# The place of the blocks' triangular inversion in the mixers' step order of a hybrid decoder layer

## The chip, the cores and the metric

The program runs on one core of one Trainium2 chip. The metric is the device time of one execution in microseconds (us); the time of the kernel before is the median of three runs. The profile is one further execution, with its own time. The engines are named as in the profile: PE multiplies matrices, PEld is PE's loading of the stationary operand, DVE and ACT do elementwise work, POOL is a slower elementwise engine, SP issues the DMAs.

## The reference

One layer of a decoder works on 1040 tokens (16 learned meta tokens and 1024 others) of width 1024, in float32:

```
h = h + 0.5 * swiglu(rmsnorm(h))                     # feed-forward 1
u = rmsnorm(h);  p = u @ w_in                        # one combined projection
o_a = gated DeltaNet(p), 8 heads of 128 x 128, chunks of tokens
o_b = RWKV-7 time mixing(p), 16 heads of 64 x 64
h = h + (sigmoid(ga) * o_a + sigmoid(gb) * o_b) @ w_out
h = h + 0.5 * swiglu(rmsnorm(h))                     # feed-forward 2
out = rmsnorm(h), without the meta tokens
```

Inside a chunk of the DeltaNet, the delta rule asks for the inverse of a unit lower triangular matrix:

```
m = where(strict, (k*beta) @ k.T * decay, 0)
tinv = inverse(m + eye)                              # triangular solve
u = tinv @ (v*beta);  wk = tinv @ (k*beta*exp(g))
step: v_new = u - wk @ S;  o = (q*exp(g)) @ S + attn @ v_new;  S = S*exp(g_last) + k_tail.T @ v_new
```

The kernel brings the RWKV branch, in the reference a scan over the tokens, into the same chunked form, so it too needs such inverses. Everything else of the mixers (projections, convolution, gates, norms) feeds these two recurrences or closes them.

## The kernel before, in words

Feed-forward 1 comes first, then the part that this case is about (function `middle`), then feed-forward 2. The middle works on two halves of the sequence: the first half has 528 columns (the 16 meta tokens and 512 others), the second 512. Each half is worked in eight steps, one for each slice of 128 channels (one DeltaNet head and two RWKV heads), so there are sixteen steps, `it` = 0 to 15. A float32 weight tile is split into a high and a low part, and each projection is three products per slice of the contraction: 24 matmuls of 512 columns, or 24 of 272 and 24 of 256 for the 528 columns of the first half (`proj`, line 307, tile `pp`).

What a step does is a list of actions in a string (lines 187 to 192): one plus sign behind a name means the action works for the step after this one, two for the step after that. For a step `it` the actions are:

- `merge_blocks`: makes 64- and 128-wide inverses from the 32-wide ones by small products on PE (lines 1619, 1627, 1638, 1643, PSUM tiles `iv`).
- `transitions`: the RWKV chunk matrices (tiles `xp`, `mp`, `np`).
- `operands+`: the next step's products of keys and queries (`grb` and `gra` on PE; `LT` and `UA` on DVE); its helper `inverse_inputs` sends the 32-wide diagonal blocks to DRAM and brings them back into `Ub`, a block to a partition.
- `inverses+`: inverts the blocks of the next step. It is 31 pairs of DVE instructions (lines 1584 and 1586, tiles `tb` and `Xb`), each of which needs the one before, and a copy `Yt` (line 1587). Then SP writes `Xb` and `Yt` to DRAM (`scX`, line 1589; `scY`, line 1591) and reads them back in another layout: `Xc` (line 1594) and `Y` (line 1598). `Xc` is what the first product of `merge_blocks` reads, `Y` what its second reads. POOL copies a part of `Xc` into `XA` as it lands (line 1600).
- `chains`: the recurrences, four chunks of 128 and eight of 64, with short hops from PE to DVE or ACT and back (lines 1742 to 1768).
- `gates`: three projections and a small product; `finish`: norms and the closing of the step, its result to DRAM (line 1828).
- `decay++`, `new_b++`, `new_a++`: the projections and first operands for the step after the next. `new_b` has three projections, and at its end the product `bon` (two matmuls of 512 columns), which DVE turns into `bv` (line 1370). `new_a` has three projections, each followed by a short convolution on DVE (line 1393, tile `acc`), by sigmoids on ACT and by norms (products `cs` with `onesr`).

The order of the instructions on each engine is fixed when the program is built: a scheduler takes the traced instructions, lets what was traced earlier go ahead where both are ready by its own estimate of durations, and writes one queue for each engine. On the chip each engine then works through its queue in this order, so PE waits where the next matmul's operand is not there, even if a later one could go. `chains`, `finish` and `inverses` use DVE together. The weight tiles (`wraw`, 512 KB each, line 260) are loaded by the same SP queue that carries the inversion's transfers; there are two raw buffers and two split ones.

Step 0's inverses are made ahead of the loop (string `FIRST`), those of step 15 in step 14 (`LAST_BUT_ONE`). The strings `REGULAR` (steps 0 to 5 and 8 to 13), `BEFORE_SWITCH` (step 6, which also begins the second half) and `SWITCH` (step 7) order the rest.

Of the kernel before, what the change touches and what calls it, by code (L numbers as in the profile page):

```python
# [170 lines left out]
def schedule():  # L171
# [5 lines left out]
    for it in range(last + 1):  # L177
        order = {NJ - 2: BEFORE_SWITCH, NJ - 1: SWITCH, last - 1: LAST_BUT_ONE, last: FINAL}.get(it, REGULAR)
        for act in order.split():
# [5 lines left out]


FIRST = "decay new_b tokens new_a decay+ operands inverses new_b+ new_a+"
REGULAR = "merge_blocks transitions operands+ inverses+ chains gates finish decay++ new_b++ new_a++"
BEFORE_SWITCH = "merge_blocks transitions operands+ inverses+ chains gates finish banks gates+ segment decay++ new_b++ tokens++ new_a++"
SWITCH = "merge_blocks transitions operands+ inverses+ chains finish decay++ new_b++ new_a++"  # L190
LAST_BUT_ONE = "merge_blocks transitions operands+ inverses+ chains gates finish"
FINAL = "gates merge_blocks transitions chains fill finish"

# [1728 lines left out]
```

## Time and profile before

| | |
|---|---|
| median of 3 runs | 3003.53 us (2999.59 to 3004.59) |
| profiled execution | 3001.24 us, span 2999.5 us, mean granted clock 0.992 |
| PE busy | 2886.0 us, 96% of the span |
| DVE busy | 2189.7 us, 73% |
| ACT busy | 1445.4 us, 48% |
| POOL busy | 491.9 us, 16% |
| the sixteen merges | first product at 865.8 us of the span, last at 2236.8 us |

How to read it: shares of busy time are means over stages. The time of an engine in one step is read from the view by windows, the start of a group and what ended the idle time before it from the timeline, and the sums of waits from the view of waits. In a timeline a row is: start, us from its first start to its last end, engine, line, operation, tiles (out<-in), shapes, count, and in brackets the engine's idle time before it with what ended it. A matmul's own duration is its time through the array; what a row of n matmuls costs PE is read from the start of the next row. A float32 matmul (`iv`, `vap`, the chains) is run as two. SPq is SP's queue: there the length of a row is how long the issuing took, not the transfer.

### The profile page before, as it was taken

How to read it: one execution, taken by the hardware profiler on the slowest of the kernel's cores; microseconds unless marked ns; L12 is line 12 of the kernel's file. 1: busy time of each engine (PE TensorE's matmuls, PEld its weight loads, DVE VectorE, ACT ScalarE, POOL GpSimd, SP SyncE). 2: the span in 40 equal slices, each digit the busy share in tenths (PEclk: the TensorE clock that was granted, in tenths of full speed). 3: DMA queues.
4: the chain of work that ended last, by engine and by line, in shares of the span. 5: the costliest groups of instructions: out<-in, count | busy, mean ns of one | idle time of the engine just before them, and what ended most of it. 6: DMA issues, size and time to landing. Idle time of an engine off the chain costs nothing. (4 is left out here: it accounts for less than half of the span.)

```text
span 2999.5 us, 62835 instructions
## 1 busy us (share of the span) xinstructions
PE 2886.0 (96%) x25630; PEld 2497.4 (83%) x25630; DVE 2189.7 (73%) x4080; ACT 1445.4 (48%) x2546; POOL 491.9 (16%) x553
## 2 busy tenths in 40 slices
PE   8999999998989999999998999999999999999998
PEld 8999999998877888888776777777787888888886
DVE  7566668876668877788867887778866666667886
ACT  5322224436555656566566556656644432223444
POOL 0332332323000000000000100000100033332431
PEclk9999999999999999999999999999999999999999
DMA  3433236553232322333332332233354332323763
GB/s 124 135 107 103 96 116 212 190 184 109 72 74 67 80 71 67 82 81 86 93 91 72 81 82 71 75 87 86 106 139 169 113 106 102 103 102 132 249 221 106
DMA packets 286849, 333.14 MB, mean 111 GB/s; under 512 B 172432, under 2 KB 178576, under 8 KB 286560
## 3 DMA queue, kind: packets, MB, share of 16 engines
q1 hardware_dynamic: 284752, 325.77, 35.6%
q8 instruction: 201, 3.29, 0.5%
q10 hardware_dynamic: 1728, 3.16, 0.3%
q14 instruction: 88, 0.72, 0.1%
q0 software_dynamic: 80, 0.19, 0.0%
HBM read 261.67 MB, written 67.38 MB: 110 GB/s over the span
## 5 line engine op out<-in xcount | busy, mean ns | idle before, releaser
L307 PE MATMUL pp<-uk,w 128*128 128x512 f32 (+2 forms) x4824 | 968.7, 346 | 9.3 <-DVE w L164 5.7
L307 PEld LDWEIGHTS pp<-uk,w 128*128 128x128 f32 x4824 | 742.8, 190 | 106.0 <-DVE w L164 13.1
L707 PE MATMUL pd<-form,w 128*128 128x256 f32 (+2 forms) x2772 | 435.0, 318 | 5.2 <-DVE w L164 4.6
L707 PEld LDWEIGHTS pd<-form,w 128*128 128x128 f32 x2772 | 395.3, 188 | 44.4 <-DVE w L164 6.7
L494 PE MATMUL pg<-bt,w 128*128 128x256 f32 (+2 forms) x2520 | 401.6, 317 | 3.0 <-DVE w L164 2.0
L164 DVE TENSOR_TENSOR w<-wraw,w 128x1024 fp32r<-128x1024 f32 (+2 forms) x266 | 346.6, 1303 | 71.7 <-ACT w L163 68.3
L494 PEld LDWEIGHTS pg<-bt,w 128*128 128x128 f32 x2520 | 360.1, 188 | 37.1 <-DVE w L164 3.1
L163 ACT ACTIVATE w<-wraw 128x1024 fp32r<-128x1024 f32 (+2 forms) x266 | 276.3, 1040 | 188.1 <-PE pg L494 116.2
L500 DVE TENSOR_TENSOR c<-c,pg 128x520 f32<-128x520 f32 (+1 forms) x280 | 189.5, 688 | 238.7 <-PE pg L494 214.7
L494 PE MATMUL pg<-b,w 128*128 128x256 f32 (+2 forms) x2160 | 347.8, 317 | 0.0
L494 PEld LDWEIGHTS pg<-b,w 128*128 128x128 f32 x2160 | 309.7, 188 | 28.1
L163 ACT ACTIVATE w<-wrx 128x1024 fp32r<-128x1024 f32 (+1 forms) x64 | 58.4, 912 | 279.8 <-PE pg L494 237.3
L464 POOL TENSOR_TENSOR wrx<-wrx 128x512 f32<-128x512 f32 x38 | 52.5, 1382 | 722.9 <-DVE w22b L164 544.9
L163 ACT ACTIVATE w<-wsum 128x768 fp32r<-128x768 f32 x96 | 75.7, 789 | 154.9 <-PE pd L707 128.8
L164 DVE TENSOR_TENSOR form<-form 128x520 fp32r<-128x520 f32 (+1 forms) x152 | 141.2, 964 | 11.0 <-ACT form L163 10.6
L164 DVE TENSOR_TENSOR w<-wsum,w 128x768 fp32r<-128x768 f32 x96 | 117.9, 1232 | 36.7 <-ACT w L163 36.7
L163 ACT ACTIVATE form<-form 128x520 fp32r<-128x520 f32 (+1 forms) x152 | 94.6, 633 | 77.6 <-DMA form<-frm 64.6
L1586 DVE TENSOR_TENSOR Xb<-Xb,tb 115x126 f32<-115x126 f32 (+22 forms) x496 | 125.4, 253 | 9.0 <-DVE rhA L1744 0.2
L242 POOL TENSOR_TENSOR wsum<-wsum,wraw 128x768 f32<-128x768 f32 (+1 forms) x48 | 98.7, 2071 | 202.7 <-DMA wraw<-in_wdn 142.0
L1584 DVE TENSOR_TENSOR tb<-Ub,Xb 115x126 f32<-115x126 f32 (+22 forms) x496 | 124.1, 250 | 8.8 <-DMA Ub<-scr 1.6
L1393 DVE SCALAR_TENSOR_TENSOR acc<-xr,pk,acc 128x528 f32<-128x528 f32 (+1 forms) x144 | 108.9, 757 | 29.2 <-ACT acc L1389 28.6
L307 PE MATMUL pwo<-uk,w 128*128 128x512 f32 x384 | 98.7, 407 | 4.1 <-ACT w L163 3.3
(424 smaller groups left out, 4381.8 us busy)
## 6 DMA issues: line engine op xcount, KB each, us to landing
wraw<-in_win SPq DMA_DIRECT2D x150, 512.0 KB
wraw<-in_wgu SPq DMA_DIRECT2D x44, 512.0 KB
wrx<-in_wgu SPq DMA_DIRECT2D x44, 512.0 KB
frm<-c SPq DMA_DIRECT2D x76, 260.0 KB
form<-frm SPq DMA_DIRECT2D x76, 260.0 KB
frm<-c SPq DMA_DIRECT2D x76, 256.0 KB
form<-frm SPq DMA_DIRECT2D x76, 256.0 KB
wraw<-in_wdn SPq DMA_DIRECT2D x40, 384.0 KB
```

Of the source, the lines that this page charges most:

```text
L163: g.nc.scalar.activation(hi, src, AF.Copy)
L164: (eng or g.nc.vector).tensor_tensor(lo, src, hi.bitcast(F32), op=ALU.subtract)
L242: g.nc.gpsimd.tensor_tensor(s, x, y, op=ALU.add if r == 1 else ALU.subtract)
L307: g.nc.tensor.matmul(ps, lhsT=l, rhs=r, start=i == 0, stop=i == n - 1)
L464: sums.tensor_tensor(a22, a21, a22, op=ALU.add)
L494: nc.tensor.matmul(ps[:, c0 : c0 + cn], lhsT=l[:, x, k, :], rhs=r[:, k, y, c0 : c0 + cn], start=i == 0, stop=i == 3 * HK - 1)
L500: nc.vector.tensor_tensor(o, x, y, op=ALU.add)
L707: nc.tensor.matmul(pd[:, c0 : c0 + cn], lhsT=wd[:, u, k - k0, :], rhs=x[:, v, c0 : c0 + cn], start=k + i == 0, stop=k == HF - 1 and i == 2)
L1393: nc.vector.scalar_tensor_tensor(acc[:, :n], xr[:, tap : tap + n], V("convw", ct * 4 + tap), acc[:, :n], op0=ALU.mult, op1=ALU.add)
L1584: nc.vector.tensor_tensor(tv, U[:, i, i + 1 :].unsqueeze(2).to_broadcast([npt, nt, ncc]), X[:, i, 0:ncc].unsqueeze(1).to_broadcast([npt, n ...
L1586: nc.vector.tensor_tensor(X[:, i + 1 :, 0:ncc], X[:, i + 1 :, 0:ncc], tv, op=ALU.add)
```

## The change

In three of the strings the word `inverses+` stands at another place. In `REGULAR` and `SWITCH` it moves from behind `operands+` to between `new_b++` and `new_a++`; in `BEFORE_SWITCH` from behind `operands+` to behind `finish`. No instruction is added or removed; the priorities by which the scheduler orders the queues change.

```
-REGULAR = "merge_blocks transitions operands+ inverses+ chains gates finish decay++ new_b++ new_a++"
-BEFORE_SWITCH = "merge_blocks transitions operands+ inverses+ chains gates finish banks gates+ segment decay++ new_b++ tokens++ new_a++"
-SWITCH = "merge_blocks transitions operands+ inverses+ chains finish decay++ new_b++ new_a++"
+REGULAR = "merge_blocks transitions operands+ chains gates finish decay++ new_b++ inverses+ new_a++"
+BEFORE_SWITCH = "merge_blocks transitions operands+ chains gates finish inverses+ banks gates+ segment decay++ new_b++ tokens++ new_a++"
+SWITCH = "merge_blocks transitions operands+ chains finish decay++ new_b++ inverses+ new_a++"
```

Three places show what this does to the queues. The merge of step 4 stands for those of steps 3 to 6, whose rows are alike, and the merge of step 12 for those of steps 10, 12 and 14.

First place, DVE, the end of the inversion for step 4 (`tb`, `Xb`, `Yt`). Before, it ends ahead of the tail of `new_b` (from `rB` on), and the row of `bv` stands fifteen rows below the last one shown:

```order
L1584 TENSOR_TENSOR tb<-Ub,Xb 115x16
L1586 TENSOR_TENSOR Xb<-Xb,tb 115x16
L1587 COPY Yt<-Xb 115x512
L1130 SCALAR_TENSOR_TENSOR rB<-pp,pk,rB 128x528
L1363 TENSOR_TENSOR AR<-rB,ELx 128x8x64
L164 TENSOR_TENSOR w<-wraw,w 128x1024
```

Now the inversion runs on through `new_b` and into the first convolutions of `new_a`. These are the rows from `bv` on:

```order
L1370 TENSOR_TENSOR bv<-bon,vB 128x512
L1584 TENSOR_TENSOR tb<-Ub,Xb 115x70
L1393 SCALAR_TENSOR_TENSOR acc<-xr,pk,acc 128x528
L1586 TENSOR_TENSOR Xb<-Xb,tb 115x5x14
L164 TENSOR_TENSOR w<-wraw,w 128x1024
L1584 TENSOR_TENSOR tb<-Ub,Xb 115x56
L1437 COPY bkpm<-bkm 64x64
L1438 COPY bkpm<-bkm 64x64
L1586 TENSOR_TENSOR Xb<-Xb,tb 115x4x14
```

and these the ones that follow them, to the end of the inversion:

```order
L1584 TENSOR_TENSOR tb<-Ub,Xb 115x45
L1586 TENSOR_TENSOR Xb<-Xb,tb 115x3x15
L1584 TENSOR_TENSOR tb<-Ub,Xb 115x30
L1397 TENSOR_TENSOR acc<-acc,xr 128x528
L1586 TENSOR_TENSOR Xb<-Xb,tb 115x2x15
L1393 SCALAR_TENSOR_TENSOR acc<-xr,pk,acc 128x528
L1584 TENSOR_TENSOR tb<-Ub,Xb 115x16
L1393 SCALAR_TENSOR_TENSOR acc<-xr,pk,acc 128x528
L1586 TENSOR_TENSOR Xb<-Xb,tb 115x16
L164 TENSOR_TENSOR w<-wraw,w 128x1024
L1587 COPY Yt<-Xb 115x512
```

The last `Xb` has moved from 19 rows ahead of `bv` to 17 rows behind it.

Second place, PE, from the second `bon` to the first product of the merge of step 4 (`iv` from `Xc`). Before:

```order
L1216 MATMUL bon<-hl,bdr 128x512
L307 MATMUL pp<-uk,w 128x256 x14
L307 MATMUL pp<-uk,w 128x272 x24
L307 MATMUL pp<-uk,w 128x256 x16
L1216 MATMUL cs<-hl,onesr 128x256
L1216 MATMUL cs<-hl,onesr 128x272
L307 MATMUL pp<-uk,w 128x256 x8
L1619 MATMUL iv_14489<-Xc,LT 32x32
```

Now:

```order
L1216 MATMUL bon<-hl,bdr 128x512
L307 MATMUL pp<-uk,w 128x256 x21
L307 MATMUL pp<-uk,w 128x272 x24
L307 MATMUL pp<-uk,w 128x256 x8
L1216 MATMUL cs<-hl,onesr 128x256
L1216 MATMUL cs<-hl,onesr 128x272
L307 MATMUL pp<-uk,w 128x256 x13
L1216 MATMUL cs<-hl,onesr 128x256
L1216 MATMUL cs<-hl,onesr 128x272
L307 MATMUL pp<-uk,w 128x256 x3
L307 MATMUL pp<-uk,w 128x512 x26
```

and behind these rows one more pair of `cs`, one `pp` of 512 columns, and the 24 products of the merge. So the whole first gate projection and three matmuls of the second (the rows of 512 columns) now stand ahead of the merge; before, they stood behind it.

Third place, PE, the same stretch for step 12, in the second half. Before:

```order
L1216 MATMUL bon<-hl,bdr 128x512
L307 MATMUL pp<-uk,w 128x512 x27
L1619 MATMUL iv_23810<-Xc,LT 32x32 x16
L1619 MATMUL iv_23810<-Xc,UA 32x32 x8
L307 MATMUL pp<-uk,w 128x512 x3
```

Now:

```order
L1216 MATMUL bon<-hl,bdr 128x512
L307 MATMUL pp<-uk,w 128x512 x26
L1216 MATMUL cs<-hl,onesr 128x512
L307 MATMUL pp<-uk,w 128x512 x4
L1216 MATMUL cs<-hl,onesr 128x512
L307 MATMUL pp<-uk,w 128x512 x14
L1619 MATMUL iv_23810<-Xc,LT 32x32 x16
L1619 MATMUL iv_23810<-Xc,UA 32x32 x8
```

Here 44 projection matmuls separate `bon` from the merge, where 27 did; on DVE the last `Xb` of this step stands three rows behind `bv`.

## The prediction

> **What bounds the kernel now.** I read the page's busy times first.
>
> ```profile
> span 2999.5 us, 62835 instructions
> PE 2886.0 (96%) x25630; PEld 2497.4 (83%) x25630; DVE 2189.7 (73%) x4080; ACT 1445.4 (48%) x2546; POOL 491.9 (16%) x553
> ```
>
> PE sets the time of the whole, so an edit that moves no work pays only by what it adds to or takes from PE's idle time. The mean over stages could hide a stage with another limit, so next comes the view by windows, from one merge to the next: steps 0 and 1, step 3 for the first half, step 11 for the second, and the switch of halves.
>
> ```profile
> core 0: us, PE busy (x) PEld busy (x) DVE busy (x) ACT busy (x) POOL busy (x), PEclk, DMA share, GB/s
> 865.80:941.10 75.30, 69.53 (x961) 63.07 (x961) 56.54 (x156) 38.58 (x83) 5.95 (x20) 0.98 0.31 71
> 941.10:1037.70 96.60, 91.99 (x1128) 78.82 (x1128) 73.73 (x183) 55.97 (x116) 5.68 (x24) 1.00 0.30 76
> 1131.90:1225.90 94.00, 90.77 (x1127) 78.89 (x1126) 72.74 (x182) 55.52 (x115) 4.49 (x22) 1.00 0.29 76
> 1608.00:1616.00 8.00, 0.45 (x1) 0.29 (x1) 8.00 (x19) 3.08 (x5) 1.12 (x3) 0.75 0.08 33
> 1889.80:1976.80 87.00, 83.94 (x943) 66.81 (x942) 70.49 (x166) 52.87 (x103) 8.19 (x15) 1.00 0.33 83
> ```
>
> A step of the first half takes 94.0 us, with PE idle for 3.2 of them; one of the second takes 87.0, with 3.1 idle. Even a perfect order of the sixteen steps would gain no more than about 50 us, while a new wait costs its full length. Only at the switch (1608 to 1616) is DVE busy all the time and PE nearly not at all. The view of waits tells whether the merge waits today:
>
> ```profile
> PE bon L1216 <- ACT hl L163: 17.8, 13, 7.6
> PE iv L1619 <- DMA Xc<-scX: 3.4, 2, 2.3
> ```
>
> (sum, count, longest). The merge's first product waited for `Xc` twice in sixteen times, 2.3 and 1.1 us (the second at the merge of step 1). How much time stands between the inversion's end and that product, the timeline shows, here at the merge of step 3:
>
> ```profile
> 1112.79 0.18 DVE L1586 TENSOR_TENSOR Xb<-Xb,tb 115x16 f32<-115x16 f32 x1
> 1113.05 1.50 SPq L1589 DMA_DIRECT2D scX<-Xb  x2
> 1114.64 3.77 SPq L1591 DMA_DIRECT2D scY<-Yt  x2
> 1118.58 2.99 SPq L1594 DMA_DIRECT2D Xc<-scX  x1
> 1123.73 1.91 SPq L1598 DMA_DIRECT2D Y<-scY  x4
> 1124.40 1.08 POOL L1600 COPY XA<-Xc 32x128 f32<-32x128 f32 x2 [4.13 <-DMA Xc<-scX]
> 1123.46 0.46 PE L1216 MATMUL bon<-hl,bdr 128*128 128x512 f32 x1
> 1123.76 6.71 PE L307 MATMUL pp<-uk,w 128*128 128x256 f32 x54
> 1130.47 0.51 PE L1216 MATMUL cs<-hl,onesr 128*128 128x256 f32 x2
> 1130.82 1.10 PE L307 MATMUL pp<-uk,w 128*128 128x256 f32 x8
> 1131.85 0.25 PE L1619 MATMUL iv<-Xc,LT 32*32 32x32 f32 x2
> ```
>
> The last `Xb` starts at 1112.79, `Xc` has landed at 1124.40 (POOL, which waited for it, starts `XA`): 11.6 us for the trip through DRAM. PE's product comes at 1131.85, 7.5 us later: that is the cover.
>
> **The change part by part.** No instruction goes or comes; the queues are ordered anew. On DVE the inversion's end moves behind `bv`; on PE more projection matmuls move ahead of the merge. Whether the merge waits is a race from the same start, the second `bon`: PE's work up to the merge against DVE's work from `bv` to the last `Xb`, plus the trip.
>
> *PE, merges of steps 3 to 6.* 69 narrow matmuls at 6.71/54 = 0.124 us are 8.6; three pairs of `cs` at 1130.82 − 1130.47 = 0.35 are 1.05; 27 of 512 columns at 0.24 (twice 0.124 is 0.25) are 6.5: 16.1 us.
>
> *DVE, the same merges.* The rows' prices are in the groups of step 3 and in a timeline of `bv`:
>
> ```profile
> L164 DVE TENSOR_TENSOR w<-wraw,w 128x1024 fp32r<-128x1024 f32 x9 | 11.0, 1219 | 1.7 <-ACT w L163 1.7
> L1586 DVE TENSOR_TENSOR Xb<-Xb,tb 115x126 f32<-115x126 f32 (+22 forms) x31 | 7.8, 252 | 0.6
> L1393 DVE SCALAR_TENSOR_TENSOR acc<-xr,pk,acc 128x528 f32<-128x528 f32 x10 | 7.6, 765 | 2.7 <-ACT acc L1389 2.7
> 1970.31 0.40 PE L1216 MATMUL bon<-hl,bdr 128*128 128x512 f32 x1
> 1970.75 0.69 DVE L1370 TENSOR_TENSOR bv<-bon,vB 128x512 f32<-128x512 f32 x1
> ```
>
> 18 rows: `bv` 0.69, one `w` 1.22, four `acc` at 0.765, ten of the inversion at 0.2 (between the group's 0.252 and 0.18 for the last `Xb`), two tiny copies at 0.1: 7.1 us. `bv` starts 0.44 us behind `bon`, which itself takes PE 0.24, so 0.2 more. From the last `Xb` to the merge there are 16.1 − 7.1 − 0.2 = 8.8 us, where step 3 had 1131.85 − 1112.79 = 19.1. The trip decides. It is longer where a weight load was issued just ahead of it, as the new queue has it, with three `wraw` in front of `scX`; the nearest case is step 1:
>
> ```profile
> 928.17 0.17 DVE L1586 TENSOR_TENSOR Xb<-Xb,tb 115x16 f32<-115x16 f32 x1
> 928.28 0.33 SPq L260 DMA_DIRECT2D wraw<-in_win  x1
> 928.71 1.86 SPq L1589 DMA_DIRECT2D scX<-Xb  x2
> 941.24 1.19 POOL L1600 COPY XA<-Xc 32x128 f32<-32x128 f32 x2 [4.94 <-DMA Xc<-scX]
> ```
>
> There it took 13.1 us. Between 11.6 and 13.1 I take 12.2. The wait is 12.2 − 8.8 = 3.4 us (2.8 to 4.3), four times: **+13.6** (11 to 17). Nothing hides it: behind the waiting product PE's queue holds projections that could run, but the order is fixed.
>
> *Merge of step 1.* 67 narrow, 47 wide, four pairs and five tiny products are 21.5 us. DVE's 30 rows (`bv`, two `w`, seven of the convolution's, one like `bv`, 17 of the inversion, two copies) are 12.8: 8.5 left, wait 3.7, of which 1.1 is there today: **+2.6**. *Merge of step 2*: 69 narrow, 21 wide, two pairs are 14.3, nine DVE rows (one `bv`, one `w`, one `acc`, four of the inversion, two copies) 3.7: 10.4 left, **+1.8** (1.2 to 2.7). *Merge of step 7* (`BEFORE_SWITCH`): the inversion ends about 25 us ahead, 0.
>
> *Merge of step 8, at the switch.* Today:
>
> ```profile
> 1621.79 0.18 DVE L1586 TENSOR_TENSOR Xb<-Xb,tb 115x16 f32<-115x16 f32 x1
> 1632.01 2.00 POOL L1600 COPY XA<-Xc 32x128 f32<-32x128 f32 x2 [17.73 <-DMA Xc<-scX]
> ```
>
> The trip takes 10.2 us. In the new order PE has 22.2 us of work from `bon` to the merge (82 wide at 0.231, the rest small) and DVE 19.1 up to the last `Xb` (three `w`, eleven of the convolution's, 26 of the inversion and three like `bv`); of DVE's some 2 overlap, since a row starts before the one ahead has quite ended. So 4 are left, and the wait is 6.2. Against it, in the saturated stretch at 1608, 17 rows of the inversion no longer stand ahead of `bv`: 17 × 0.2 = 3.4 us less. **+2.8** (−1 to 5).
>
> *Merges of steps 9 to 14.* Step 12 today:
>
> ```profile
> 1959.57 0.17 DVE L1586 TENSOR_TENSOR Xb<-Xb,tb 115x16 f32<-115x16 f32 x1
> 1966.99 1.49 POOL L1600 COPY XA<-Xc 32x128 f32<-32x128 f32 x2 [0.89 <-DMA Xc<-scX]
> 1968.36 0.50 PE L1216 MATMUL bon<-hl,bdr 128*128 128x512 f32 x1 [1.48 <-ACT hl L163]
> 1970.55 6.30 PE L307 MATMUL pp<-uk,w 128*128 128x512 f32 x27
> 1976.78 0.75 PE L1619 MATMUL iv<-Xc,LT 32*32 32x32 f32 x32
> ```
>
> The trip is 7.4 us here. Now 44 wide matmuls at 6.23/27 = 0.231 and two pairs come to 10.7; DVE's three rows ahead of the last `Xb` to 1.7: 8.8 left after the 0.2, for merges 10, 12, 14. Merges 11 and 13 come to 10.0, merge 9 to 7.4. At 7.4 none waits; at 10.2 (the switch's trip) five-odd microseconds in all. I take **+2** (0 to 6), nearer to the second half's own row.
>
> *What gets better.* `bon` waits 1.48 us in such a step for a chain through DVE and ACT; fewer rows of the inversion stand ahead of it, two of 0.2: **−2.4** in six steps (−9 to 0).
>
> *Chains.* In the first half the scheduler puts narrower pieces between the recurrence's hops:
>
> ```profile
> 1924.33 0.39 PE L1742 MATMUL p<-SA,kq 128*128 128x128 f32 x2
> 1925.24 0.38 PE L1748 MATMUL p<-rhA,Y 128*128 128x128 f32 x2
> ```
>
> The hop takes 0.91 us. In chunks three and four three matmuls of 272 columns and a small product now stand in it, 0.73 with the hop's own two: about 0.2 short, two or three times a step, 0.5 × 6 = **+3** (0 to 6).
>
> *The clock.* The row of step 0 has PE idle for 5.8 us, a clock of 0.98: 2% of 75.3 is 1.5 us. Step 1 idles 4.6 us with 1.00. A wait of 3.4 can be followed by a stretch at a lower clock: seven waits at 0 to 1.7, **+4** (0 to 12), a third. Beside this row stands a rule: the Trainium skill, "TensorE: Matmul & The Clock Gate", Part 1, says that the array drops to half clock after at least one idle window of some 3.4 us, and that the window runs freely. By that rule a wait of 3.4 barely fills a window, so this term would be 0 and the sum 4 lower.
>
> Sum: 13.6 + 2.6 + 1.8 + 2.8 + 2 − 2.4 + 3 + 4 = +27.4. The profiled execution took 3001.24 us, 2.3 below the median and inside the three runs' spread: 3028.6, so I forecast 3029. All terms at one end together would give some 3005 and 3054; since they don't move together, the case's own range is 3012 to 3050.
>
> **The rivals.** *Faster* (no waits, relief stays). If the trip falls below 8.8 us in the first half, no merge of steps 3 to 6 waits; what is left is the switch's 3.4, the 2.4 at `bon` and the 1.5 at the clock: −7.3, **2994**. For it: the second half's 7.4. Against: the trips of 11.6 and 13.1, with SP's issues alone from 1113.05 to past 1118.58. The Trainium skill, "DMA: Bandwidth & Descriptors", Anatomy of one DMA, gives about 2.0 us fixed for a DMA (fitted on another path); two in series would be an estimate of some 4 us, and this rival would hold. The rows of this case, 7.4 to 13.1, disagree.
>
> *No change.* The trip is 9 to 10, waits of 1 are paid for by the relief: 3 to 7 us either way, **3002**. For it: DVE may run the late inversion faster than in order of my rows, since `acc` waits on ACT there (2.7 us a step); that also cuts against it.
>
> *Much slower.* SP's queue works in order. In the new order `scX` to the `ym` behind it hold it for some 14 us (in step 3 the rows of SP run from 1113.05 to beyond 1125), and the second gate's weights are loaded only then. If they come late by 5 us in six steps, +30 on top: **3056**. Against: PE needs them some 28 us after `Xb`, by the same prices. It decides if a load takes over 14 us from its issue.
>
> **How the numbers follow.** The waits at the merges (3029) have a chance of 0.67: DVE's and PE's rows are counted, the trip has three measured lengths, and all those of the first half exceed 8.8. Faster 0.15, no change 0.13, much slower 0.05. A measurement tells 0.2%, 6 us, from no change. Faster takes its whole case; the same and slower theirs: 0.15, 0.13, 0.72. The range runs from 2998, where no more than a tenth lies below, to 3050, the forecast's upper end; the likeliest case alone has 3012 to 3050.
>
> **What would show it.** Right: PE's wait of `iv` on `Xc` grows from 3.4 us to some 22 in the view of waits, with 2.8 to 4.3 in each of the merges 3 to 6; the last `Xb` starts 7 to 8 us behind the second `bon`; step 3's window grows from 94.0 to about 98. The waits of `bon` shrink, those at the hops grow. Wrong: `XA` within 9 us of `Xb` in the first half (faster, or no change); waits of PE at `pp` for `w` behind the merge (much slower); or a last `Xb` well over 8 us behind `bon`, which would make each wait longer than summed.

## The result and the profile after

The kernel changed takes 3019.74 us (median, 3018.46 to 3021.77), the kernel before 3004.06 in the same series: a ratio of 1.0054 with a 95% interval of 1.0037 to 1.007. The change makes the program some 16 us slower. The forecast was 3029 us: the sign and the main place (the merges of the first half) were right, the size was too large by 9 us.

The page of the profiled execution after:

```profile
span 3017.0 us, 62823 instructions
PE 2898.1 (96%) x25630; PEld 2508.8 (83%) x25630; DVE 2189.7 (73%) x4080; ACT 1451.7 (48%) x2546; POOL 484.0 (16%) x553
```

The span has grown by 17.5 us. PE is idle for 118.9 us where it was for 113.5, only 5.4 more; the other 12.1 us are in PE's *busy* time, at the same 25630 matmuls. So, net of what was won elsewhere, less than a third of the loss is waiting; in the rest PE worked more slowly. The view by windows shows where, in steps 3, 4 and 5, from merge to merge:

```profile
core 0: us, PE busy (x) PEld busy (x) DVE busy (x) ACT busy (x) POOL busy (x), PEclk, DMA share, GB/s
1143.70:1241.90 98.20, 93.61 (x1128) 80.28 (x1128) 72.84 (x181) 56.85 (x115) 3.97 (x22) 0.98 0.29 74
1241.90:1338.40 96.50, 91.97 (x1128) 79.26 (x1128) 72.74 (x181) 56.84 (x115) 3.98 (x22) 1.00 0.29 74
1338.40:1436.50 98.10, 93.53 (x1128) 80.44 (x1129) 72.47 (x179) 56.45 (x114) 3.93 (x22) 0.98 0.28 72
```

A step of the first half took 94.0 us; now it takes 96.5, or 98.1 where the mean clock in it was 0.98. In the second half two successive steps differ, since the merges stand at alternating places, but four of them (1824.7 to 2172.5) take 347.8 us together, 87.0 each, as before. The view of waits on PE (sum, count, longest):

```profile
PE pp L307 <- DVE w L164: 15.1, 22, 3.2
PE bon L1216 <- ACT hl L163: 12.5, 13, 3.9
PE iv L1619 <- DMA Xc<-scX: 9.5, 7, 2.1
PE iv L1638 <- DVE XA L1634: 5.1, 6, 1.5
PE vbp L1269 <- DVE vB L1130: 3.1, 1, 3.1
```

The merge's first product waits seven times, 9.5 us in all, where it waited twice, 3.4 in all. The waits of `bon` have lost 5.3 us, 3.7 of them at the switch of halves; the waits of projections for a split weight (`pp` for `w`) have grown by 9.4. The merge waits a second time, too: its later products from `XA` (line 1638) stood for 5.1 us, six times, where they stood for 0.6 once. The merge of step 3, in the timeline:

```profile
1125.43 0.40 PE L1216 MATMUL bon<-hl,bdr 128*128 128x512 f32 x1
1125.95 0.68 DVE L1370 TENSOR_TENSOR bv<-bon,vB 128x512 f32<-128x512 f32 x1
1132.23 0.17 DVE L1586 TENSOR_TENSOR Xb<-Xb,tb 115x16 f32<-115x16 f32 x1
1132.47 1.50 SPq L1589 DMA_DIRECT2D scX<-Xb  x2
1134.09 3.74 SPq L1591 DMA_DIRECT2D scY<-Yt  x2
1138.00 2.99 SPq L1594 DMA_DIRECT2D Xc<-scX  x1
1143.78 0.60 POOL L1600 COPY XA<-Xc 32x128 f32<-32x128 f32 x2 [5.42 <-DMA Xc<-scX]
1142.10 0.50 PE L307 MATMUL pp<-uk,w 128*128 128x512 f32 x1 [0.29 <-DVE w L164]
1143.70 0.75 PE L1619 MATMUL iv<-Xc,LT 32*32 32x32 f32 x32 [1.10 <-DMA Xc<-scX]
```

The last `Xb` now starts 6.8 us behind `bon`, the trip through DRAM takes 11.6 us as it did before, and PE, which has nothing else in its queue's order, stands for 1.10 us. Merges 3 to 6 are alike (1.09 to 1.16), those of steps 1 and 2 wait 1.22 and 1.73.

Behind some waits the clock falls. The trace's record of the clock has seven stretches at half clock from 850 to 2300 us, each 3.41 or 6.83 us long, where the profile before has three; within a profile their starts are whole multiples of 3.413 us apart (1145.41 and 1339.97: 57 of them). Windows cut at these marks, around the merges of steps 3 and 4:

```profile
1142.00:1145.41 3.41, 2.21 (x52) 1.65 (x53) 1.34 (x3) 1.49 (x4) 0.56 (x2) 1.00 0.97 153
1145.41:1148.82 3.41, 3.41 (x9) 2.66 (x9) 2.55 (x8) 3.34 (x8) 0.77 (x3) 0.50 0.45 68
1237.57:1240.98 3.41, 2.94 (x13) 1.94 (x11) 3.37 (x6) 3.35 (x6) 0.00 (x0) 1.00 0.61 82
1240.98:1244.40 3.42, 2.52 (x54) 2.13 (x55) 1.53 (x5) 1.56 (x5) 1.27 (x5) 1.00 0.69 137
```

At step 3 PE was idle for 1.20 us of a window of 3.41, and the next 3.41 us ran at a clock of 0.50: 1.7 us lost. At step 4 a wait just as long fell on two windows, which had 0.47 and 0.90 us idle, and the clock stayed at 1.00. Summed as (1 − clock) × length from 850 to 2300, the profile before lost 6.8 us to the clock and this one 17.1: 10.2 more, most of the growth in PE's busy time. Only 6.8 of the 17.1 stand behind waits at merges (stretches from 961.1, 1145.4 and 1340.0; 1.7 before). The others follow PE's waits for a split weight (923.6), at `vbp` (1538.0), at the `bon` of the switch (1626.7) and in the recurrence (1684.7).

A profile is one execution. By the mean granted clock of each run, the four executions of the change lost 33 us over the whole program, those of the kernel before 26: some 7 to 8 us more.

### The profile page after: what moved, and what is told of

The parts are those of the page before. It is cut to its first block, busy times and chain, and to the rows that moved or that the text cites. A ratio compares the mean times of both kernels' runs of the same rounds, so it can differ in the third digit from the quotient of the medians.

```text
span 3017.0 us, 62823 instructions
## 1 busy us (share of the span) xinstructions
PE 2898.1 (96%) x25630; PEld 2508.8 (83%) x25630; DVE 2189.7 (73%) x4080; ACT 1451.7 (48%) x2546; POOL 484.0 (16%) x553
## 4 chain that ended last, share of the span: by engine, by line
PE 46%; DVE 15%; ACT 3%; DMA 2%; issue 2%; SPq 1%; DVEq 0%; ACTq 0%
PE pg L494 11%; PE pp L307 11%; PE pd L707 7%; DVE w L164 2%; PE pwo L307 2%; DVE tb L1584 2%; DVE Xb L1586 2%; PE pg L518 1%; PE xp L1269 1%; DVE acc L1393 1%; DMA Xc<-scX 1%; PE vp L1269 1%; PE gra L1470 1%; PE bkt L1501 1%; PE mp L1269 1%
## 5 line engine op out<-in xcount | busy, mean ns | idle before, releaser
L307 PEld LDWEIGHTS pp<-uk,w 128*128 128x128 f32 x4824 | 751.2, 191 | 119.9 <-DVE w L164 23.1
L494 PE MATMUL pg<-b,w 128*128 128x256 f32 (+2 forms) x2160 | 347.8, 317 | 0.0
```

The costliest lines, as they stand in the source:

```text
L307: g.nc.tensor.matmul(ps, lhsT=l, rhs=r, start=i == 0, stop=i == n - 1)
L494: nc.tensor.matmul(ps[:, c0 : c0 + cn], lhsT=l[:, x, k, :], rhs=r[:, k, y, c0 : c0 + cn], start=i == 0, stop=i == 3 * HK - 1)
```

## The experiments

The theory after the two traces, **A**: the loss is made in the first half; the merges wait there, and half-clock stretches behind the waits cost more than the waits. Its rivals are **B** (the first half loses only its waits, 6 us, the switch and the second half the rest), **W** (the clock falls anyway, only the waits would be won back) and **O** (the order of the queues costs by itself). All kernels ran five rounds beside the kernel before.

### Which steps

Three kernels carry the new strings only in some steps. The edit, in `schedule` (EARLY holds the three strings of before; the other two runs have 8 to 13, and 6 and 7):

```
-        order = {NJ - 2: BEFORE_SWITCH, ...}.get(it, REGULAR)
+        order = {NJ - 2: BEFORE_SWITCH, ...}.get(it, REGULAR); order = order if it in (0, 1, 2, 3, 4, 5) else EARLY.get(order, order)
```

> The strings of the change only in steps 0 to 5 (the merges of steps 1 to 6); steps 6 to 14 as before. Theory A (the loss is made in the first half, by the waits at its merges and by half-clock stretches behind them; in the traces the projections' product bon of step 6 is 12.4 us later than before, and the end 17.5): 3004.1 + 13 = 3017 us (3012 to 3022), the view of waits with 8 to 10 us at iv for Xc. Theory B (the waits at the merges, 6 us more than before, are all that the first half loses; the rest is made at the switch and in the second half): 3010 us (3007 to 3012).

> The strings of the change only in steps 8 to 13 (the merges of steps 9 to 14); everything ahead as before. Theory A: no merge waits there (trips of 7.2 to 9.1 us against 9 to 12 of cover), the step keeps 87.0 us, so 3004 us (3001 to 3008), with the waits of bon 1.0 us less a step and waits of pp for w in their place. Theory B: 3009 us (3007 to 3012).

> The strings of the change only in steps 6 and 7 (the merges of steps 7 and 8). Theory A: the stall of 7.6 us at the bon of the switch shrinks to some 4, and a wait of 3.1 us at vbp and half-clock stretches give it back: 3004 us (3000 to 3008). Theory B: 3009 us (3006 to 3012). A third way: the relief stays without the wait, 3000 us.

Measured: first half 3020.24 us, ratio 1.0051 (1.0034 to 1.0068); second half 3001.25, 1.0002 (0.9988 to 1.0016); switch 3000.1, 0.9991 (0.9974 to 1.0008). The whole loss is in the first half's six steps; B is out. The profile of the first-half run has the waits of the change again, that of the switch run has the relief at `bon` (17.8 before). One row of each:

```profile
PE iv L1619 <- DMA Xc<-scX: 9.6, 7, 1.8
```

```profile
PE bon L1216 <- ACT hl L163: 12.7, 12, 4.0
```

At the switch the relief is there, 3.6 us, without the wait at `vbp` that theory A expected: the time is that of the third way, yet the run is not distinguishable from the kernel before.

The fourth run of this series moves the inversion half as far:

```
-REGULAR = "merge_blocks transitions operands+ inverses+ chains gates finish decay++ new_b++ new_a++"
+REGULAR = "merge_blocks transitions operands+ chains gates inverses+ finish decay++ new_b++ new_a++"
```

> inverses+ between gates and finish in REGULAR (in the other two just ahead of finish too): later than before by the chains and gates, earlier than in the change by finish, decay and new_b. Counted from the queues, 12.8 to 15.7 us stand between the last Xb and the merge for steps 3 to 6 and 15.4 for steps 10 to 14, both over the trips of 11.4 and 7.3, so those merges do not wait; only those of steps 1 and 2 (10.0 and 8.5) can. Theory A: 2998 to 3006 us. Theory B (an inversion that runs through later work costs by itself, without a wait at the merge): 3009 us or more.

Measured: 3005.5 us, 1.0007 (0.9996 to 1.0019): no loss that can be told from zero. Its merges of steps 3 to 6 do not wait (cover left: 1.0 to 1.9 us). Steps 4 and 5 take 93.0 us each in its profile, less than the 94.0 of before; the three waits at its merges 0 to 2 (4.1 us, where the kernel before has 3.4) and its stretches at low clock give this back. So moving the inversion later does not cost by that alone. This kernel's queues differ from the change's in more than the cover, though; the next runs keep them.

### The wait taken away and added, with the queues' order kept

Why does the trip (from here on counted from the end of the last `Xb`) take 11.4 us in the first half and 7.3 in the second? Up to `Xc` the instructions are the same but for one size: `scY` is written from 51 rows of `Yt` in the first half (three blocks belong to the meta tokens), from 48 in the second. Writing other numbers of rows leaves the order of PE, DVE and ACT as it is, instruction by instruction, so these runs change only the trip and what queues behind it.

With 48 rows in every step:

```
-    nblk = NBLK + 3 * meta
+    nblk = NBLK
...
-        ymv = scY[NBLK:, 0:8].rearrange("t c r i -> (c r) t i")
+        ymv = scY[0:3, 0:8].rearrange("t c r i -> (c r) t i")
```

and with 51 rows in every step:

```
-    nblk = NBLK + 3 * meta
+    nblk = NBLK + 3
```

> The change with one size altered: scY is written from 48 rows of Yt in every step, where the first half writes 51 (the three blocks of the meta tokens are left out, and ym reads the first three blocks in their place, so the output is not the reference's). All queues keep the order of the change. In its trace the write of 51 rows runs at some 33 GB/s and holds Xc behind it (trip 11.4 us), the one of 48 in the second half at over 100 (trip 7.3). Theory A (waits at the merges of the first half, and half-clock stretches behind them): the trip falls to 7 to 8.5, the waits of iv for Xc go from 9.5 us to under 1, and most of the stretches at 956 to 1345 go: 3020 - 16 = 3004 us (3000 to 3008). Theory W (only the waits themselves count, the clock drops anyway, for the small products of the merge stand with less work between them): 3011 us (3009 to 3013). Theory O (the order of the queues costs by itself): 3016 us or more.

> The same alteration in the kernel before (same omission). Its merges wait only at steps 0 and 1, 3.4 us in all. All theories: those go, 3004 - 3.4 - 1 = 2999 us (2996 to 3003); the time shows how much of the former run's gain is not due to the change.

> The change with 51 rows of Yt written to scY in the second half too (nothing is left out); all queues keep the order of the change. If the 51 rows make the long trip, those of steps 8 to 15 go from 7.2 to 9.3 us to about 11.4, over a cover of 9 to 10.5: waits of 1.5 to 3.4 us at eight merges, some 14 us. Theory A: with half-clock stretches behind half of them, 3020 + 14 + 6 = 3040 us (3033 to 3048). Theory W: 3034 us. If the length of the trip has another cause: 3020 us.

Measured: the change with 48 rows 3003.61 us, 1.0001 (0.9991 to 1.0011); the kernel before with 48 rows 3000.67, 0.9989 (0.9977 to 1.0); the change with 51 rows everywhere 3043.39, 1.0133 (1.0115 to 1.015). Theory A expected 3004, 2999 and 3040. The first run excludes W and O as they were stated: with 48 rows no merge waits for `Xc`, from 950 to 1600 there is no stretch at half clock, and by the granted clock its twelve executions lost 24 us, no more than the kernel before. What is left to the order of the queues comes below. With 51 rows everywhere the merges of the second half wait too, 1.35 to 2.19 us each, and the view of waits has

```profile
PE iv L1619 <- DMA Xc<-scX: 22.5, 15, 2.2
```

13 us more of waits than in the change, for 23.7 us more of time; by the granted clock another 9 us are lost to it (43 in place of 33). Not all waits are followed by a drop of the clock: four steps of that half (1838.1 to 2191.8) take 353.7 us where the change took 347.8, 1.5 us more each, just the wait, at a clock of 1.00.

The 48-row runs leave work out. A complete form puts the tiles on 128 partitions and writes 64 rows in the first half:

```
-    npt = 115
-    nblk = NBLK + 3 * meta
+    npt = 128
+    nblk = 64 if meta else NBLK
```

> The change, complete, with Ub, Xb, tb and Yt on 128 partitions in place of 115, and 64 rows of Yt written to scY in the first half in place of 51 (48 in the second half as before). PE, DVE and ACT keep the order of the change. If what is slow about the 51 rows is how they are spread over the DMA engines, 64 rows are fast, the trip is 7.5 to 9 us and the waits at the merges go as with 48: 3004 us (3000 to 3008). If it is that more rows take longer: 3020 us or more.

> The same alteration, complete, in the kernel before: the waits of 3.4 us at the merges of steps 0 and 1 go, as with 48 rows: 3000 us (2997 to 3003).

Measured: 3007.47 us, 1.0013 (1.0004 to 1.0023), and 2999.59, 0.999 (0.9982 to 0.9999). Again no merge waits for `Xc`, and the granted clock says 25 us lost. But against the kernel before with the same rows the change still costs 7.9 us, with 48 rows 2.9. So of its 15.7 us, 8 to 13 go with the long trip and 3 to 8 with the order of the queues: theory A holds for half of it or more, and O has a share that these pairs do not pin down.

More rows are faster than 51, so it is not that they are many that makes the write slow. The merge of step 4 in the profile of the change with 64 rows (`scY` in 1.66 us of issue where it took 3.74, `Xc` in 0.39 where it took 2.99):

```profile
1228.88 1.53 SPq L1589 DMA_DIRECT2D scX<-Xb  x2
1230.50 1.66 SPq L1591 DMA_DIRECT2D scY<-Yt  x2
1233.22 0.39 SPq L1594 DMA_DIRECT2D Xc<-scX  x1
1236.58 0.99 POOL L1600 COPY XA<-Xc 32x128 f32<-32x128 f32 x2 [1.82 <-DMA Xc<-scX]
```

and the rate of all transfers during the trip, in 40 equal slices (GB/s), first of the change from 1132.4 to 1143.8 us, then of the change with 64 rows from 1228.4 to 1236.3:

```profile
GB/s 0 0 0 0 16 97 106 93 100 115 96 72 41 35 35 35 33 33 32 33 33 33 31 33 33 32 33 33 33 32 32 33 57 159 199 204 142 140 223 144
```

```profile
GB/s 0 0 0 0 0 0 0 0 1 84 97 106 107 85 101 108 107 102 110 127 160 146 123 98 164 183 153 134 27 12 111 103 181 217 233 323 259 180 207 92
```

With 51 rows some 20 slices of 0.285 us, nearly 6 us, run at a third of the rate of the others, and `Xc` is queued behind them; with 64 rows nothing of that is left. The same two views give the mean busy share of the 16 DMA engines, in tenths:

```profile
DMA  0000189899863222333333223333333349999699
DMA  0000000007899899999999879998206699999994
```

In the slow slices the engines are busy for two to three tenths of the time, in the writes beside them for seven to nine. So most of them stand idle at any time there, which fits the expectation that it is the spread of the 51 rows over the engines; which engine carried which rows, no run shows.

### Controls, and one that went wrong

> The kernel before with 51 rows written in the second half too. Trips of steps 9 to 14 go from 7.3 to about 11.4 us under a cover of 17: hidden. The merges of steps 8 and 15, with 0.7 and 0.8 us to spare, can wait 1 to 3 us each. Theory A (a long trip costs only where the merge waits for it): 3007 us (3003 to 3011). If a long trip costs by holding the queue for the weights behind it: 3015 us or more.

The kernel before with 51 rows in both halves: 3008.57 us, 1.0014 (1.0004 to 1.0024). Its trips of steps 9 to 14 grow from 7.3 to 11.3 us, and those merges still don't wait (5.4 to 5.8 us to spare); only those of steps 8 and 15 do, 1.36 and 2.63 us. A trip that is 4 us longer costs nothing where PE has work ahead of the merge. In the change the same lengthening cost 23.7 us.

The other complete way to a short trip was to write 48 rows and then 3:

```
-        nc.sync.dma_start(scY[:nblk, :, r, :], Yt[64 * r : 64 * r + nblk])
+        nc.sync.dma_start(scY[:NBLK, :, r, :], Yt[64 * r : 64 * r + NBLK])
...
-        ymv = scY[NBLK:, 0:8].rearrange("t c r i -> (c r) t i")
+        ymv = scY[NBLK:, 0:8].rearrange("t c r i -> (c r) t i"); [nc.sync.dma_start(scY[NBLK:, 0:8, r, :], Yt[64 * r + NBLK : 64 * r + nblk, 0:8]) for r in range(2)]
```

> The kernel before with the write of 51 rows made as one of 48 and, behind the reads of Y, one of 3 rows (8 of the 16 columns, all that is read): nothing is left out. The scheduler orders the first half anew for it; counted from the queues, 10.2 to 18.9 us stand between the last Xb and the merges of steps 1 to 6, all over a trip of 7.5. All theories: no waits at the merges, 3000 us (2996 to 3004).

Measured: 3016.01 us, 1.0033 (1.0021 to 1.0046). The expectation failed, though its premise held: the first half's trips are 7.7 to 9.5 us and no merge waits for `Xc`. Two more DMAs in a step made the scheduler order the first half anew, and PE now waits elsewhere, among others for weights that DVE or ACT has yet to split (5.7 and 0.7 before):

```profile
PE pp L307 <- DVE w L164: 8.1, 6, 3.2
PE pp L307 <- ACT w L163: 5.5, 4, 2.9
```

Its profile loses 18.8 us to the clock from 850 to 2300, about as much as that of the change (17.1). Which part of its new order is to blame was not tried.

> Complete: the strings of the change only in steps 6 and 7, with the 64 rows. At the switch the stall at bon shrinks from 7.6 to 4.0 us, and the waits at the first two merges go: 3004 - 3.6 - 3.4 = 2997 us (2993 to 3001).

Measured: 3000.18 us, 0.9988 (0.9978 to 0.9998). The 64 rows are worth some 4 us to the kernel before (2999.59); the new strings at the switch add nothing that can be told. Both complete kernels are a tenth of a per cent faster than the kernel before, with intervals that end just under 1.

## Why the prediction was right, and where its sum was off

**The mechanism held.** The inversion ends behind `bon`, the cover no longer reaches over the trip, and the merges of steps 1 to 6 wait. Taking the trip's excess away with the queues as they are brings 16.1 us back (48 rows) or 12.3 (64 rows), of which the kernel before gains 3.9 or 4.6 as well.

**That the sum came so near is in part luck.** It was 27.4 us where 15.7 were measured. The merges of steps 1 to 6 came to 6.3 and not 18.0; the clock came to 7 to 10 and not 4; the merge's second wait and one at `vbp`, 4.5 and 3.1 us, are not in it. Errors of opposite signs cancelled in part. Of the signs that the prediction named, a step of about 98 us came (96.5 to 98.2), but in part by the clock; some 22 us of `iv` on `Xc`, with 2.8 to 4.3 at each merge, did not come (9.5 and 1.1).

**Merges of steps 3 to 6** were priced at 13.6 us and cost 4.5. Cover and trip were both a little off, and the wait is their difference. DVE needed 6.3 us from `bv` to the start of the last `Xb`, not 6.9 (7.1 with that row itself: a row starts some 0.1 us before the long one ahead of it has ended, and the sum added whole durations). PE's stretch between `bon` and the merge took 16.9 us, not 16.1 (`pp` waited 0.5 us for `w` in it). So the cover was 10.4 and not 8.8. The trip was 11.6 from the start of the last `Xb`, as the prediction counts it, the low end and not 12.2: three weights ahead of it in the queue did not lengthen it. An error of 2.3 us in quantities of 9 to 17 took two thirds of a term that is their difference.

**Merges of steps 1, 2, 7** were priced at 2.6, 1.8 and 0, and came to 0.1, 1.7 and 0. **The switch** was priced at +2.8, a wait of 6.2 against 3.4 of relief. The stall at `bon` fell from 7.6 to 3.9, as summed, but the merge did not wait. Its trip was 7.8 us, not 10.2, and its cover 9.8, not 4: PE took 28.0 us from `bon` to the merge where 22.2 were summed. (The prediction's own numbers, 22.2 − 19.1 + 2, leave 5.1 and not 4.)

**A wait of 3.1 at `vbp`** (1536.6, ahead of the merge of step 7) was in no term. It is the slow write again: a small load, `rsA`, stands behind `Xc` in SP's queue, and DVE waits for it,

```profile
1533.28 1.22 DVE L1171 TENSOR_TENSOR_SCAN c<-rsA,lm 8x512 f32<-8x512 f32 x1 [2.56 <-DMA rsA<-in_ck]
```

two rows ahead of the `vB` that `vbp` needs. With 48 or 64 rows the wait is 0.7.

**Merges 9 to 14** don't wait at all (+2 predicted): the trips stay at 7.2 to 9.1. **Waits of `bon`** in those steps fell by 1.6, −2.4 predicted.

**The clock** was priced at +4, a third of what seemed possible, and cost about 10 in this profile, 7 to 8 by the granted clock of all runs. It stood behind other waits as well as those at the merges, and with the trip of 48 or 64 rows that cost is gone (24 and 25 us lost, 26 in the kernel before). The rule weighed beside it (the Trainium skill, "TensorE: Matmul & The Clock Gate", Part 1: half clock after at least one idle window of some 3.4 us, in a window that runs freely) would have made it 0. The trace disagrees on the first half of the rule: 1.20 and 1.33 us of idle time in the 3.41 us ahead were enough at steps 3 and 5. It agrees with the second: the stretches start on marks of 3.413 us that the waits do not shift, and the same wait at steps 4 and 6, split by such a mark, had no effect. Idle time alone does not decide, though: at the merge of step 2 a window had 1.73 us of it (1043.01 to 1046.42), and the clock stayed at 1.00.

**The order of the queues** was priced at +3, in the chains' hops. In the change with 64 rows, where nothing waits for `Xc`, a step takes

```profile
1334.50:1429.90 95.40, 91.87 (x1129) 79.26 (x1128) 72.63 (x180) 56.52 (x115) 4.52 (x22) 1.00 0.28 74
```

So a step of the first half is 94.0 us before, 95.4 with the new order alone, 96.5 with the wait of 1.1, and 98.1 with a half-clock stretch behind it. The 1.4 us of the order are real (7.9 us a run with 64 rows, 2.9 with 48), but hardly lie in the hops: over the whole run PE's waits in the recurrences are 5.5 us before and 6.0 after. In this step PE is idle for 0.3 us more than in step 3 of before and busy for 1.1 more, at a clock of 1.00. The idle time has changed places. The merge's products from `XA` now wait, in the change with 64 rows as in the change,

```profile
PE iv L1638 <- DVE XA L1634: 4.6, 6, 1.0
```

0.7 us in each of the merges 3 to 6: between the merge's first products and these stand 17 projection matmuls where 26 stood (merge of step 4), for the others are now ahead of the merge. That would explain the wait; no run tried it alone. Waits elsewhere in the step have shrunk by nearly as much. Of the busy time, projections take 0.8 us more, the sums `cs` 0.4, the recurrences' products 0.3. Why the same matmuls take longer at these places was not settled.

**The rivals.** *Faster* needed a trip under 8.8 us in the first half. The runs with 48 and 64 rows gave it one of 7.4 to 9.2, and the change was then no faster than the kernel before: this rival was wrong in its price too, having no term for what the order costs by itself. The figure beside it (the Trainium skill, "DMA: Bandwidth & Descriptors", Anatomy of one DMA, about 2.0 us fixed) gave an estimate of some 4 us for two in series; the trace disagrees, the shortest trip took 7.2 us. *No change* would have been right with 48 rows; with 64 the change costs 7.9 us against its like. *Much slower* did not happen: the weights behind the trip came in time, and from step 0 on the waits of `pp` for `w` are short ones of 0.2 to 0.8 us, but for one of 2.6. Of its mechanism, the queue held by the trip, only the wait at `vbp` came true.

## What to carry to other kernels

Price a wait as the difference of two counted stretches, and give it the error of both; then add what PE loses at a lower clock behind it, which here was some 7 to 10 us beside 6 of waits for `Xc`. Count also what stands inside the moved stretch: here fewer projections were left within the merge, and it waited a second time. Before moving work because a transfer is long, ask why it is long: here one number of rows made it 4 us longer, and with another number in both kernels the same move of the inversion cost 3 to 8 us in place of 16. To test such a cause under a scheduler, change a size that leaves the queues' order as it is; an edit that adds two DMAs was undone by the order that came with it.

## What the runs showed of the hardware

A write of 51 rows of 2 KB to DRAM (in pieces of 128 bytes) ran at 33 GB/s for most of its time, with the 16 DMA engines busy for two to three tenths; writes of 48 and 64 rows ran at about 100, with seven to nine tenths. The DMA issued behind the slow write took 2.99 us to issue, not 0.39.

Stretches at half clock lasted 3.41 or 6.83 us and started on a grid of 3.413 us (961.10, 1145.41 and 1339.97 in the profile after). Idle time of 1.20 to 2.02 us in the 3.41 us ahead went before each of the seven from 850 to 2300, so a window need not have been idle throughout; but a window with 1.73 us idle was also followed by full clock, so idle time is not all that counts. What else counts is open.
